# A feed-forward stage whose resident matmul operands lie at four offsets within 256 bytes

## The chip, the cores and the metric

The kernel runs on one core of one Trainium2 chip. The metric is the device time of one execution in microseconds; the median of several executions counts. Everything is float32 in the interface; the large matmuls run on operands that are split into a rounded high part and a remainder.

## The reference, cut to what matters

One encoder layer of width 1024 over 2048 positions. A mixer (convolution, gated recurrence and chunked attention side by side) comes first, then a gated feed-forward part of inner width 2816. The change lies in the feed-forward part alone:

```
mod = (c_act @ w_ada[l] + b_ada[l])[:, None, :]
sh1, sc1, g1, sh2, sc2, g2 = jnp.split(mod, 6, axis=-1)
...
x = layer_norm(ALPHA * x + (1.0 + g1) * y, ln1_g[l], ln1_b[l])
h = x * (1.0 + sc2) + sh2
gt, up = jnp.split(h @ w_ffn_in[l], 2, axis=-1)
y = (jax.nn.silu(gt) * up) @ w_ffn_out[l]
x = layer_norm(ALPHA * x + (1.0 + g2) * y, ln2_g[l], ln2_b[l])
```

## The kernel before

The program is traced as one long list of instructions with priorities, and a scheduler orders it on each engine; semaphores and places in memory are given by the same layer. The mixer takes the 2048 positions in four stretches of 512. Its projections are in `proj_f` (line 270: weights `whl` stationary, the input `hh`/`hl` moving, 512 columns) and `proj_t` (line 321: `hh`/`hl` or the mixer's output `yh`/`yl` stationary, weights `whl` moving, 256 columns).

Every float32 product is made of three matmuls, in the order of `PASSES`: high by high, high by low, low by high. A matmul names two operands in the core's memory: the stationary one (128 columns, loaded by its own weight load while the matmul before it streams) and the moving one (512 columns here, streamed through the array).

The feed-forward part has two stages.

- **First stage, `ffn_in` (line 953).** For each of two halves `g` of the positions and each of 22 blocks `f` of the inner width, seven products (a fast scheme for a 2 by 2 block product) are formed. Each product runs over four inner blocks `idx` and three passes, so a block has 7 x 4 x 3 = 84 matmuls and the stage 44 x 84 = 3696. The moving operands are `oph` and `opl`, the split activations; they stay resident for all 22 blocks of a half. The stationary operands are `fhi` and `flo`, the split weights, renewed for each block.
- **Second stage, `ffn_out` (line 1095).** For each of two halves `dh` of the output columns and each group `ts` of four (at the end two) blocks of positions, 22 inner blocks `f` are summed. The moving operands are the split output weights, which take the same tiles `oph`/`opl` through `load_op`, with `f % 4` as index; the stationary ones are `ahi`/`alo`, the split activations (for a few of the last group, `oph`/`opl` tiles as well).

`op_tiles` (line 853) asks for the resident tiles: one tag for each `idx` and part, with seven buffers of 2 KB per partition each, in the pool `p1`, which lies at the upper end of the memory and is filled from `idx` 0 upwards. The pools `st` (staging of the first stage) and `p2` (of the second) lie right below `p1`, `pw` (weights, `fhi`, `flo`, `fraw`, `fu`) lies at the lower end. All tiles here are a multiple of 512 bytes, so within one pool all start at the same offset modulo 256 bytes, as the built program gives them:

```
tiles                        offset modulo 256, before
oph, opl  (all 56 buffers)   224
fhi, flo, ahi, alo           160
st: opraw, h2, fraw0, xst    224
whl, hh, hl (mixer)          224
yh, yl (mixer)               192
```

The slices that a matmul reads within these tiles begin at multiples of 512 bytes, so these numbers hold for every matmul of lines 270, 321, 953 and 1095.

Of the kernel before, what the change touches and what calls it, by code (L numbers as in the profile page):

```python
# [7 lines left out]
F32 = mybir.dt.float32  # L8
# [7 lines left out]
P = 128  # L16
# [17 lines left out]
NK, NG = KT // 2, 2  # L34
# [74 lines left out]
def mixer_phase(tc, es, env):  # L109
# [681 lines left out]
    for q in range(NQ):  # L791
# [25 lines left out]
        if q + 1 == NQ:  # L817
            for _ in rest:
                pass
            as_.close()  # L820
            rs_.close()
            ffn_open(tc, env)
        else:
            nxt = fronts_a(q + 1)
# [7 lines left out]

def ffn_open(tc, env):
    pf = env["pf"] = ExitStack()
    env["p1"] = pf.enter_context(tc.tile_pool(name="p1", bufs=1, side="right", reuse_waits="tile"))
    st = env["st_es"] = ExitStack()
    env["st"] = st.enter_context(tc.tile_pool(name="st", bufs=1, side="right", reuse_waits="tile"))
    env["actd"] = [tc.dram_tile([P, NG * 2 * Q], F32, name=f"actd{f}") for f in range(NF)]
    env["ops"] = load_ops(tc, env, 0, range(2))
# [13 lines left out]
def op_tiles(env, idx):  # L853
    p1 = env["p1"]
    hi = p1.tile([P, Q], F32R, name="oph", tag=f"oph{idx}", bufs=7)
    lo = p1.tile([P, Q], F32R, name="opl", tag=f"opl{idx}", bufs=7)
    return hi, lo
# [10 lines left out]
def load_ops(tc, env, g, ns=range(7)):  # L868
    return {(n, idx): load_op(tc, env, env["srcd"][g][n * NK + idx], idx, env["st"], "h2", N_H2)
            for n in ns for idx in range(NK)}  # L870
# [344 lines left out]
```

## Time and profile before

| what | value |
|---|---|
| median of 3 runs | 2593.28 us (2588.7 to 2594.78) |
| the profiled execution | 2589.91 us |
| its span | 2588.2 us, granted clock 0.974 in the mean |
| PE busy | 2457.8 us, 95% of the span |
| DVE, ACT, POOL busy | 64%, 39%, 26% |
| the chain that ended last | PE 78%, of which line 953 31% and line 1095 17% |

Busy time of PE counts a matmul from its start to the end of its drain, and matmuls overlap. How fast they follow each other is read from the distance of their starts, in the timeline or from a count over a stretch without waits.

### The profile page before, as it was taken

How to read it: one execution, taken by the hardware profiler on the slowest of the kernel's cores; microseconds unless marked ns; L12 is line 12 of the kernel's file. 1: busy time of each engine (PE TensorE's matmuls, PEld its weight loads, DVE VectorE, ACT ScalarE, POOL GpSimd, SP SyncE). 2: the span in 40 equal slices, each digit the busy share in tenths (PEclk: the TensorE clock that was granted, in tenths of full speed). 3: DMA queues.
4: the chain of work that ended last, by engine and by line, in shares of the span. 5: the costliest groups of instructions: out<-in, count | busy, mean ns of one | idle time of the engine just before them, and what ended most of it. 6: DMA issues, size and time to landing. Idle time of an engine off the chain costs nothing.

```text
span 2588.2 us, 36360 instructions
## 1 busy us (share of the span) xinstructions
PE 2457.8 (95%) x13274; PEld 2078.5 (80%) x13274; DVE 1656.1 (64%) x2917; ACT 997.2 (39%) x1920; POOL 665.7 (26%) x571
## 2 busy tenths in 40 slices
PE   6888899999999999987999999999999999999998
PEld 5766799879977898876878788888888888888887
DVE  7987696669557785666655555765445474364666
ACT  2444444354244433544323333433333352242333
POOL 3433112200152112510333332332322211111121
PEclk8997999999999999988999999999999999999999
DMA  9676667663755645547333332442222274454544
GB/s 354 212 236 187 186 197 264 201 180 128 241 183 172 205 164 184 191 135 259 102 117 119 118 130 90 164 142 91 74 82 90 74 244 142 130 182 134 161 147 142
DMA packets 202691, 423.99 MB, mean 164 GB/s; under 512 B 20240, under 2 KB 69008, under 8 KB 202512
## 3 DMA queue, kind: packets, MB, share of 16 engines
q1 hardware_dynamic: 202352, 421.15, 49.8%
q8 instruction: 104, 1.70, 0.3%
q14 instruction: 75, 0.61, 0.1%
q0 software_dynamic: 160, 0.52, 0.1%
HBM read 317.78 MB, written 95.42 MB: 160 GB/s over the span
## 4 chain that ended last, share of the span: by engine, by line
PE 78%; DVE 10%; DMA 6%; issue 3%; ACT 2%; POOL 1%; SPq 0%; DVEq 0%; POOLq 0%; ACTq 0%
PE pi L953 31%; PE po L1095 17%; PE pjt L270 11%; PE pjt L321 9%; PE lp L513 2%; DVE cacc L377 2%; PE sc L625 1%; PE tp L661 1%; PE tp L648 1%; DMA whl<-wki 1%; DMA whl<-wko 1%; PE lp L533 1%; DMA xst<-zall 1%; DMA opraw<-srcd 1%; DMA xb<-in_x_dram 1%
## 5 line engine op out<-in xcount | busy, mean ns | idle before, releaser
L953 PE MATMUL pi<-oph,fhi 128*128 128x512 f32 x1232 | 484.1, 393 | 17.8 <-ACT fhi L829 11.9
L953 PE MATMUL pi<-opl,fhi 128*128 128x512 f32 x1232 | 483.7, 393 | 0.0
L953 PE MATMUL pi<-oph,flo 128*128 128x512 f32 x1232 | 478.9, 394 | 0.0
L270 PE MATMUL pjt<-hh,whl 128*128 128x512 f32 x1184 | 402.5, 411 | 16.2 <-DMA whl<-wki 6.4
L953 PEld LDWEIGHTS pi<-oph,fhi 128*128 128x128 f32 x1232 | 232.4, 189 | 70.2 <-ACT fhi L829 12.1
L829 ACT CAST fhi<-fraw 128x512 fp32r<-128x512 f32 x220 | 136.2, 621 | 392.3 <-PE pi L953 376.6
L270 PEld LDWEIGHTS pjt<-hh,whl 128*128 128x128 f32 x1184 | 227.4, 194 | 66.4 <-DMA whl<-wki 6.0
L958 DVE TENSOR_TENSOR fu<-fu,pi 128x512 f32<-128x512 f32 x176 | 120.8, 686 | 245.8 <-PE pi L953 245.1
L953 PEld LDWEIGHTS pi<-opl,fhi 128*128 128x128 f32 x1232 | 232.5, 189 | 52.3
L1095 PE MATMUL po<-oph,alo 128*128 128x512 f32 (+1 forms) x702 | 273.9, 390 | 0.0
L1095 PE MATMUL po<-oph,ahi 128*128 128x512 f32 (+1 forms) x702 | 270.1, 385 | 3.1 <-DVE res L1116 3.1
L1095 PE MATMUL po<-opl,ahi 128*128 128x512 f32 (+1 forms) x702 | 272.6, 388 | 0.0
L953 PEld LDWEIGHTS pi<-oph,flo 128*128 128x128 f32 x1232 | 232.3, 189 | 49.5 <-DVE flo L830 0.2
L830 DVE TENSOR_TENSOR alo<-araw,ahi 128x512 fp32r<-128x512 f32 x172 | 148.5, 871 | 190.9 <-ACT ahi L829 174.3
L270 PE MATMUL pjt<-hl,whl 128*128 128x512 f32 x592 | 243.0, 411 | 0.0
L321 PE MATMUL pjt<-whl,yh 128*128 128x256 f32 x1024 | 196.7, 288 | 15.5 <-DMA whl<-wko 12.0
L830 DVE TENSOR_TENSOR flo<-fraw,fhi 128x512 fp32r<-128x512 f32 x220 | 159.5, 742 | 70.9 <-ACT fhi L829 70.8
L377 DVE SCALAR_TENSOR_TENSOR cacc<-u,cs,cacc 128x512 f32<-128x512 f32 x240 | 195.3, 843 | 0.2
L829 ACT CAST ahi<-araw 128x512 fp32r<-128x512 f32 x172 | 104.9, 618 | 222.3 <-PE po L1095 208.0
L321 PEld LDWEIGHTS pjt<-whl,yh 128*128 128x128 f32 x1024 | 164.1, 194 | 17.7 <-DVE yl L231 7.9
L930 POOL TENSOR_TENSOR ft<-fraw 128x512 f32<-128x512 f32 x43 | 59.9, 1392 | 450.6 <-DMA fraw<-in_w_fi_dram 433.5
L1095 PEld LDWEIGHTS po<-oph,ahi 128*128 128x128 f32 x702 | 132.4, 189 | 31.7 <-DVE res L1116 3.3
(257 smaller groups left out, 4539.1 us busy)
## 6 DMA issues: line engine op xcount, KB each, us to landing
whl<-wki SPq DMA_DIRECT2D x156, 512.0 KB, 3.8
fraw<-in_w_fi_dram SPq DMA_DIRECT2D x86, 512.0 KB, 3.7
araw<-actd SPq DMA_DIRECT2D x154, 256.0 KB, 3.4
wki<-whl SPq DMA_DIRECT2D x52, 512.0 KB, 4.3
whl<-wko SPq DMA_DIRECT2D x48, 512.0 KB, 3.5
actd<-fs SPq DMA_DIRECT2D x44, 512.0 KB, 3.3
xb<-in_w_ada_dram SPq DMA_DIRECT2D x64, 256.0 KB, 4.7
opraw<-srcd SPq DMA_DIRECT2D x56, 256.0 KB, 5.0
```

The source lines that it names most:

```text
L270: nc.tensor.matmul(out=ps[j], lhsT=w[kt // 2][a][:, kt % 2, j * P:(j + 1) * P], rhs=hts[kt][c], start=(kt == 0 and n == 0), stop=(kt == KT ...
L321: nc.tensor.matmul(out=ps[tt // 2][:, tt % 2, :], lhsT=lhs[2 * kp + k][c][:, tt * P:(tt + 1) * P], rhs=w[kp][a][:, k, :], start=(ko == 0 a ...
L377: nc.vector.scalar_tensor_tensor(out=ac, in0=us[j][:, t:t + Q], scalar=col(wc + t), in1=ac, op0=ALU.mult, op1=ALU.add)
L513: nc.tensor.matmul(out=lp[0:n, c, :], lhsT=ddf[:, c * P:c * P + n], rhs=d4[:, c, :, :], start=True, stop=True)
L533: nc.tensor.matmul(out=lp[:, c, :], lhsT=K[:, 2 * i + c, :], rhs=M[:, 2 * i + c, :], start=True, stop=True)
L625: nc.tensor.matmul(out=sc[:, 0:n + x], lhsT=qs[hd][ph][:, i * P:(i + 1) * P], rhs=kt_[:, o - x0:o - x0 + n + x], start=ph == 0, stop=ph == 1)
L829: nc.scalar.copy(out=hi, in_=src)
L830: nc.vector.tensor_tensor(out=lo, in0=src, in1=hi.bitcast(F32), op=ALU.subtract)
L930: e.tensor_tensor(out=t1, in0=w12, in1=w11, op=ALU.subtract)
L953: nc.tensor.matmul(out=out, lhsT=w[n][a][:, idx, :], rhs=ops[n, idx][c], start=first and idx == 0 and i == 0, stop=idx == NK - 1 and i == ...
L958: nc.vector.tensor_tensor(out=out, in0=a, in1=b, op=ALU.add)
L1095: nc.tensor.matmul(out=pts[j][:, c], lhsT=a[x][:, j * P:(j + 1) * P], rhs=wo[f][y][:, c], start=f == 0 and m == 0, stop=f == NF - 1 and m ...
```

## The change

In `ffn_open` the pool `p1` is filled in an order and with spacers written out by hand. For each `idx` its two tags are asked for once, before their first use; ahead of `idx` 1, 2 and 3 stands a tile of 32 bytes per partition, and after the last a tile of 128 bytes. Nothing reads or writes the spacers, nor the eight tiles asked for here.

```
 def ffn_open(tc, env):
     pf = env["pf"] = ExitStack()
-    env["p1"] = pf.enter_context(tc.tile_pool(name="p1", bufs=1, side="right", reuse_waits="tile"))
+    p1 = env["p1"] = pf.enter_context(tc.tile_pool(name="p1", bufs=1, side="right", reuse_waits="tile"))
+    for idx in range(NK):
+        if idx:
+            p1.tile([P, 8], F32, name=f"gap{idx}")
+        op_tiles(env, idx)
+    p1.tile([P, 32], F32, name="gap")
     st = env["st_es"] = ExitStack()
```

In the built program the pool grows by 3 x 32 + 128 = 224 bytes, downwards:

```
tiles                        before   after   (modulo 256)
oph, opl, idx 0              224      0
oph, opl, idx 1              224      32
oph, opl, idx 2              224      64
oph, opl, idx 3              224      96
fhi, flo, ahi, alo           160      160
st: opraw, h2, fraw0, xst    224      0
```

Each engine has the same instructions on the same operands in the same order as before. One wait is new: the third GpSimd operation of the first weight block (line 937 before, `fraw0` in `st`) also waits for the last attention matmul of the mixer (line 661), since the pool `st` now overlaps other old tiles.

## Rows read from the trace of the kernel before

**Rows 1.** The page: busy time of each engine, and shares of the last chain.
```profile
PE 2457.8 (95%) x13274; PEld 2078.5 (80%) x13274; DVE 1656.1 (64%) x2917; ACT 997.2 (39%) x1920; POOL 665.7 (26%) x571
PE pi L953 31%; PE po L1095 17%; PE pjt L270 11%; PE pjt L321 9%; PE lp L513 2%; DVE cacc L377 2%; PE sc L625 1%; PE tp L661 1%; PE tp L648 1%; DMA whl<-wki 1%; DMA whl<-wko 1%; PE lp L533 1%; DMA xst<-zall 1%; DMA opraw<-srcd 1%; DMA xb<-in_x_dram 1%
```
**Rows 2.** Windows: stretch, length, busy time (instructions) by engine, granted clock, DMA.
```profile
1500.00:2100.00 600.00, 600.00 (x2630) 492.04 (x2629) 327.94 (x454) 212.63 (x363) 178.66 (x125) 1.00 0.33 113
```
**Rows 3.** Chain of work that ended last: start us, us, what.
```profile
1536.83 549.61 PE pi L953 x2400
...
2095.13 427.81 PE po L1095 x1869
```
**Rows 4.** Waits from 1500 us to 2588 us: waiter, awaited, us, times, longest.
```profile
ACT fhi L829 <- PE pi L953: 344.9, 187, 2.1
...
DVE fu L958 <- PE pi L953: 180.7, 83, 4.0
```
**Rows 5.** The same stretch, waits of PE alone.
```profile
PE po L1095 <- DVE res L1116: 3.1, 1, 3.1
```
**Rows 6.** Counts: windows of line 953 and 1095; casts into oph; groups by shape.
```profile
1227.00:2095.00 868.00, 855.16 (x3696) 695.65 (x3696) 0.99 0.33 112
...
2086.20:2580.50 494.30, 485.95 (x2178) 401.09 (x2178) 1.00 0.51 159
...
L829 ACT CAST oph<-opraw x100: 602/620/627, 1189.4 to 2323.0; 128x512 fp32r<-128x512 f32 x100
...
L1095 PE MATMUL po<-oph,ahi 128*128 128x256 f32 x28 | 8.6, 306 | 3.1 <-DVE res L1116 3.1
...
L1095 PE MATMUL po<-opl,oph 128*128 128x256 f32 x16 | 4.5, 282 | 0.0
```
**Rows 7.** Timeline of PE in line 953: start us, us, engine, line, what.
```profile
1700.13 0.39 PE L953 MATMUL pi<-oph,flo 128*128 128x512 f32 x1
...
1700.82 0.39 PE L953 MATMUL pi<-oph,flo 128*128 128x512 f32 x1
```
**Rows 8.** Timeline of PE in line 270, from the end of a wait.
```profile
851.94 0.50 PE L270 MATMUL pjt<-hh,whl 128*128 128x512 f32 x1 [0.47 <-DMA whl<-wki]
852.28 0.40 PE L270 MATMUL pjt<-hl,whl 128*128 128x512 f32 x1
...
854.61 0.62 PE L270 MATMUL pjt<-hh,whl 128*128 128x512 f32 x2
...
858.68 0.39 PE L270 MATMUL pjt<-hh,whl 128*128 128x512 f32 x1
```
**Rows 9.** Line 270 in a stretch of matmuls without a wait.
```profile
809.12 0.39 PE L270 MATMUL pjt<-hl,whl 128*128 128x512 f32 x1
...
817.28 0.39 PE L270 MATMUL pjt<-hl,whl 128*128 128x512 f32 x1
```
**Rows 10.** Timeline of PE in line 321, stationary yh and yl.
```profile
384.07 0.40 PE L321 MATMUL pjt<-whl,yh 128*128 128x256 f32 x2
...
384.77 0.40 PE L321 MATMUL pjt<-whl,yh 128*128 128x256 f32 x2
```
**Rows 11.** Timeline of PE in line 321, stationary hh and hl.
```profile
890.98 0.40 PE L321 MATMUL pjt<-whl,hh 128*128 128x256 f32 x2
...
891.70 0.40 PE L321 MATMUL pjt<-whl,hh 128*128 128x256 f32 x2
```
**Rows 12.** GpSimd at the first weight block: timeline, and its sequencer's wait.
```profile
1230.45 2.20 POOL L937 TENSOR_TENSOR fraw<-fraw,ft 128x512 f32<-128x512 f32 x1 [7.01 <-issue]
...
L937 POOLq EVENT_SEMAPHORE  x1: 7612/7612/7612, 1222.7 to 1222.7; - x1
```
**Rows 13.** The last attention matmuls (chain), and transposes of the first stage (line 889).
```profile
1179.73 1.29 PE tp L661 x20
...
L889 PE MATMUL tp<-ident,xst x64: 270/272/273, 1285.4 to 1536.6; 128*128 128x128 f32 x64
```

## The prediction

> **What bounds the kernel now.** I read the page first: PE is busy 95% of the span, and lines 953 and 1095, the two stages whose moving operands are moved in memory, hold 31% and 17% of the last chain [rows 1]. Is PE there the bound, or does it only happen to be late? From 1500 to 2100 us it is busy 600.00 of 600.00 us at a granted clock of 1.00, the 2.4 GHz level, while DVE, ACT and GpSimd are busy 328, 213 and 179 us [rows 2]. The waits of that stretch to the end run the other way: ACT and DVE wait for PE's matmuls (344.9 and 180.7 us in the first stage alone) [rows 4], PE itself for one result of DVE, 3.1 us [rows 5]. So what a matmul costs there goes to the end one for one, and a faster or slower matmul finds nothing that hides it: the other engines have slack on the fast side, and on the slow side they wait longer.
>
> How long is a matmul? Not its 388 to 394 ns in the groups, which include the drain, but the distance of starts. The chain gives it: 2400 matmuls of line 953 in 549.61 us, 229.0 ns each, and 1869 of line 1095 in 427.81 us, 228.9 ns [rows 3]. The timeline shows the same close up: three matmuls, one of each pass, in 0.69 us [rows 7]. At the full clock 512 columns need 512 / 2.4 = 213.3 ns. **So 15.6 ns of each matmul, 6.8%, are spent on something else than columns, though nothing is waited for.** That is the only thing that this change can touch.
>
> **Is it a matter of addresses?** The trace of before has two comparisons. First, line 321, where only the stationary operand differs: with `yh`/`yl` (offset 192) six matmuls of 256 columns take 0.70 us, 116.7 ns each [rows 10]; with `hh`/`hl` (offset 224, like the moving `whl`) they take 0.72 us, 120.0 ns [rows 11]. The code, shapes and clock are the same, the offset modulo 256 isn't. Second, line 270, where both operands lie at 224: 36 matmuls of 512 columns in 8.16 us, 226.7 ns [rows 9], against 228.9 in line 953 with 224 moving and 160 stationary. So an effect of 2 to 3 ns per matmul comes with the pair of offsets, of the order of a matmul's overhead, not of its length. I take it that the two reads, the moving one and the next weight load, which overlap, disturb each other, and that it depends on where they begin; the trace shows the difference, not the cause.
>
> A third reading speaks of how it sets in. In line 270, just behind a DMA wait, the first ten matmuls from 852.28 to 854.61 us are 233 ns apart, and the eighteen from there to 858.68 us 226 ns [rows 8]. The pattern needs some ten matmuls to settle.
>
> The Trainium skill speaks against the change here: "SBUF — State Buffer", section "Who interferes with whom", gives TensorE two independent read ports, one for the moving operand and one for the weight load, and says that TensorE never waits on anyone. By that page offsets would do nothing; the 116.7 against 120.0 ns do not agree with it, at least not without another cause. Its result is a rival below.
>
> **The change, part by part.**
>
> *The moving operands of line 953.* 3696 matmuls [rows 6], from 224 to 0, 32, 64 and 96 by inner block; the stationary ones stay at 160, so the difference of the two (moving less stationary) goes from 64 to 96, 128, 160 and 192 modulo 256. No row has these pairs. The nearest rows are 226.7 ns (difference 0) and 228.9 ns (difference 64, now), at 512 columns; the present pair is the worse of the two that are known in a settled state. The bounds are 213.3 ns, columns alone, and the unsettled 233 ns. I take 226.7, the value that a settled pattern at another difference has here: 3696 x 2.2 = 8.1 us less.
>
> *The moving operands of line 1095.* 2178 matmuls [rows 6]. In the last group some are of 256 columns: 28 for each of three pairs of names with `ahi`/`alo`, 16 for each of three with `oph`/`opl` as stationary operand, 132 in all [rows 6], so 2046 are full. The output weights use the same tiles, with f modulo 4 as index, so they move as well. 2046 x 2.2 = 4.5 us less. The 132 half-width ones change by 3.3 ns at most by rows 10 and 11: 0.4 us either way, left out.
>
> *The pool below.* `st` and `p2` go from 224 to 0. They feed casts of ACT (100 at 620 ns in the whole stage [rows 6]) and DVE, which lie under PE, and 64 transposes of line 889 [rows 13]; even 3 ns on each of those would be 0.2 us. Nothing.
>
> *The eight extra tiles and four spacers.* No instruction belongs to them; the buffers' turn begins one further, and the resident operands' waits stay. Nothing.
>
> *The new wait.* GpSimd's third operation on the first weight block starts at 1230.45 us, after its sequencer had stood for 7.6 us from 1222.7 us; the matmul that it must now also wait for ended by 1181.0 us [rows 12, 13]. The wait is met 40 us before. Queued behind it on GpSimd are this operation and the next of the block, and ACT's cast for PE's third product waits on them; an extra sequencer instruction there costs a fraction of a microsecond, below the rounding of the sum. If this cover were gone, the whole front of line 953 would stand.
>
> The sum is 8.1 + 4.5 = 12.6 us. From the profiled execution, 2589.91 us, that gives 2577.3 us. The median shown lies 3.4 us higher; against it the time is 2580.7 us, and that is what I give.
>
> **The rivals.**
>
> *Unsettled (slower).* In line 953 the offset now changes after every three matmuls, in line 1095 after every twelve or six. If a change of offset starts the pattern afresh as a wait does in rows 8, it never settles in 953 and hardly in 1095. Between the 231 ns that a half-settled pattern would have and the 233 of the first ten lies +2.1 to +4.1 ns on 5742 matmuls: 12 to 24 us slower, 2605 to 2617 us. It decides from the point where the mean passes 229 ns. For it: the change of offset every 0.7 us, and three of the four new differences are unlike any that has a row. Against it: in rows 8 a gap in the stream went ahead, and here there is none. The same time would come from differences that settle badly.
>
> *Nothing (same).* The offsets don't matter in this pairing, because the cost is per matmul, or because four differences average out to what one costs today. Then 2593 us, within 5 us. This is also what the Trainium skill's two independent ports say, on the page named above. For it: 228.9 and 226.7 lie only 1% apart, so averaging could well end between them. Against: the 3.3 ns between rows 10 and 11.
>
> *Much better (faster).* The present 15.6 ns are for the most part a clash of the two reads, and the new differences keep them apart, so that a matmul comes near its columns: 224 to 216 ns, 5 to 13 ns on 5742, 29 to 75 us less, 2518 to 2564 us. For it: all moving operands of 512 columns in this trace begin at 224, so none that begins at 0 or 64 was ever seen, and the overhead is large. Against it: no row at all below 226.
>
> [...]
>
> **How the numbers follow.** The forecast, 226.7 ns with about 1.2 ns to each side (6 to 19 us faster, 2574 to 2587 us): 0.38. Much better: 0.15. Nothing: 0.20. Unsettled: 0.27. Faster by over 0.2% (5 us, about what a measurement of this kernel can tell from no change) is the first two, 0.53; within it 0.20; slower 0.27. The range goes to half of the strong gain (41 us, 221.7 ns: 2552 us) and to 19 us on the slow side (232.2 ns: 2612 us), which leaves out some 0.08 on either end. The likeliest case's own range is 2574 to 2587 us.
>
> **What would show it.** In the profile after, line 953's chain row: 2400 matmuls in 544 us mean that the forecast's size is right, 549 us that nothing happened, 556 us or more that the pattern stays unsettled, 530 us that the reads really were in each other's way. Lines 270 and 321 must not change at all, since their operands don't move: if they do, it is not the offsets. In the timeline of line 953 the distances should repeat every twelve matmuls, as the offset goes round. The front at 1230 us should stand where it does. I am wrong in the mechanism if 953 and 1095 move in opposite directions by much, and in the sign if the four offsets cost more in passing from one to the next than each saves.

## Result: slower by 0.7%, and the profile after

| | before | changed |
|---|---|---|
| median of 3 runs | 2593.28 us | 2607.78 us (2604.8 to 2611.15) |
| ratio | 1 | 1.0067, 95% interval 1.0048 to 1.0086 |
| span of the profiled execution | 2588.2 us | 2609.4 us |

The forecast was 2580.7 us, faster; the kernel is 14.5 us slower by the medians. The range of 2552 to 2612 us holds the time, the sign is the other one. The spans differ by more than the medians, 21.2 us: the profiled execution of the changed kernel is the slowest of its three, and single executions of one kernel scatter. Of the kernel before, 24 executions beside the first experiments lie between 2580.73 and 2599.31 us, with a median of 2589.84 us, 17.9 us below the changed kernel. How fast the matmuls follow each other is therefore read from the traces, where it repeats far more closely: 549.61 and 549.35 us for 2400 matmuls in before and in e4 below, which have the same offsets there.

PE is still what everything waits for. The stretch from 1500 to 2100 us of the changed kernel answers to [rows 2]: stretch, length, busy time of PE, weight load, DVE, ACT and GpSimd, granted clock, DMA share, GB/s.

```profile
1500.00:2100.00 600.00, 600.00 (x2593) 485.37 (x2592) 319.24 (x440) 203.14 (x346) 171.30 (x121) 1.00 0.31 106
```

The clock is the same full 2.4 GHz level and PE is busy throughout, but 2593 matmuls stand where 2630 stood. To the end of the program PE waits once, as in [rows 5]:

```profile
PE po L1100 <- DVE res L1121: 1.5, 1, 1.5
```

The chain of the changed kernel (start us, us, what; lines 958 and 1100 are 953 and 1095 of before) answers to [rows 3]:

```profile
1544.03 557.38 PE pi L958 x2400
...
2110.24 447.31 PE po L1100 x1917
```

557.38 / 2400 = 232.2 ns and 447.31 / 1917 = 233.3 ns between starts, where before had 229.0 and 228.9. The sum by the prediction's own counts is 3696 x 3.2 + 2046 x 4.4 = 11.8 + 9.0 = 20.8 us, against 21.2 us between the two spans. So nearly the whole loss between the two spans stands in the two stages, in matmuls that wait for nothing.

The front is where it was. The chain and the sequencer's rows of GpSimd in the changed kernel answer to [rows 12, 13]:

```profile
1180.67 1.29 PE tp L661 x20
...
1230.91 2.12 POOL fraw L942
```
```profile
L942 POOLq EVENT_SEMAPHORE  x2: 17/30/43, 1230.7 to 1230.8; - x2
```

The last attention matmuls end at 1182.0 us, and the operation that now also waits for them starts at 1230.91, against 1230.45 us before: the new wait costs nothing.

### The profile page after: what moved, and what is told of

The parts are those of the page before. It is cut to its first block, busy times and chain, and to the rows that moved or that the text cites. A ratio compares the mean times of both kernels' runs of the same rounds, so it can differ in the third digit from the quotient of the medians.

```text
span 2609.4 us, 36361 instructions
## 1 busy us (share of the span) xinstructions
PE 2476.6 (95%) x13274; PEld 2075.0 (80%) x13274; DVE 1656.4 (63%) x2917; ACT 997.5 (38%) x1920; POOL 666.0 (26%) x571
## 4 chain that ended last, share of the span: by engine, by line
PE 75%; DVE 13%; DMA 7%; issue 2%; ACT 2%; POOL 1%; SPq 1%; DVEq 0%; ACTq 0%; POOLq 0%
PE pi L958 31%; PE po L1100 18%; PE pjt L270 10%; PE pjt L321 7%; DVE cacc L377 3%; PE lp L513 2%; PE sc L625 1%; DMA xb<-in_w_ada_dram 1%; PE tp L661 1%; PE tp L648 1%; DMA whl<-wki 1%; DMA xst<-zall 1%; DVE tmp L496 1%; DVE tmp L297 1%; PE lp L533 1%
## 5 line engine op out<-in xcount | busy, mean ns | idle before, releaser
L958 PE MATMUL pi<-oph,fhi 128*128 128x512 f32 x1232 | 488.8, 397 | 19.6 <-ACT fhi L829 13.1
L958 PE MATMUL pi<-opl,fhi 128*128 128x512 f32 x1232 | 490.3, 398 | 0.0
L958 PEld LDWEIGHTS pi<-opl,fhi 128*128 128x128 f32 x1232 | 233.1, 189 | 54.4
```

The lines of the kernel that those rows point to most:

```text
L958: nc.tensor.matmul(out=out, lhsT=w[n][a][:, idx, :], rhs=ops[n, idx][c], start=first and idx == 0 and i == 0, stop=idx == NK - 1 and i == ...
```

## Experiments: which pair of offsets, and what a passing costs

Two explanations were open: the passing from one offset to the next (the prediction's slower rival), or each new pair of offsets by itself. All twelve kernels have the instructions of before in the same order on each engine; only places in memory differ (and the new wait, where the pools `st` and `p2` move). A difference below is the moving operand's offset less the stationary one's, modulo 256 bytes.

### One offset instead of four

Experiment e1 keeps the changed kernel's pool and its size, without the spacers between the inner blocks, so that all lie at 0.

```
-    env["p1"] = pf.enter_context(tc.tile_pool(name="p1", bufs=1, side="right", reuse_waits="tile"))
+    p1 = env["p1"] = pf.enter_context(tc.tile_pool(name="p1", bufs=1, side="right", reuse_waits="tile"))
+    for idx in range(NK):
+        op_tiles(env, idx)
+    p1.tile([P, 56], F32, name="gap")
```

> The four inner blocks lie at one offset, 0 modulo 256, for moving operands; the stationary ones stay at 160; staging is at 0 as in the changed kernel. Theory 'pair' (the time of a matmul is set by the offsets of its two operands, and settles at once): both stages at 233 ns between starts, as line 1095 of the changed kernel has within its runs of twelve at offset 0, so 15 to 25 us slower than before. Theory 'unsettled' (the passing from one offset to the next costs): 227 to 229 ns, within 12 us below or level with before.

Measured: 2610.29 us, ratio 1.0077 (1.0052 to 1.0102). Its chain:

```profile
1540.79 560.00 PE pi L956 x2400
...
2109.66 447.54 PE po L1098 x1918
```

233.3 ns in both stages, with nothing to pass between. So a passing is not needed for the loss: the pair of offsets alone brings it.

### The stationary operands moved to the moving ones

Experiment e2 leaves the resident operands at 224 and puts 64 bytes ahead of the split weights (the other tiles of `pw` behind them move along).

```
     pw.tile([P, 2, NK, P], F32, name="fraw", tag="fraw", bufs=N_RAW)
+    pw.tile([P, 16], F32, name="wgap")
```

> The kernel before with a spacer of 64 bytes ahead of the split weights: moving operands at 224, stationary at 224 instead of 160. Theory 'difference' (what counts is the difference of the two offsets, as line 270 with 224 and 224 shows): 226.7 ns in both stages, 12 to 13 us faster than before. Theory 'start of the moving operand' (only that offset counts): 228.9 ns, no change.

Measured: 2576.78 us against 2589.84 us of before beside it, ratio 0.9951 (0.9935 to 0.9967).

```profile
1530.55 544.04 PE pi L953 x2400
...
2083.21 423.65 PE po L1096 x1869
```

544.04 / 2400 = 226.7 and 423.65 / 1869 = 226.7 ns, as line 270 in [rows 9]. The gain is 3696 x 2.3 + 2046 x 2.2 = 13.0 us by the chain and 13.1 us by the medians. This is the size of gain that was forecast for the change (12.6 us), from an edit that makes the two offsets equal.

Experiment e3 puts both at 0: e1 with a `wgap` of 24 floats as in e2.

> Moving operands of all four inner blocks at 0 and the stationary ones at 0 as well. Theory 'difference': the difference is 0 as in line 270, so 226.7 ns and 12 to 13 us faster than before. Theory 'start of the moving operand': 0 is the bad place, so 233 ns and 15 to 25 us slower, as with all at 0 and the stationary ones at 160.

Measured: 2576.72 us, ratio 0.9948 (0.9929 to 0.9967).

```profile
1528.58 544.05 PE pi L956 x2400
...
2081.24 423.65 PE po L1099 x1869
```

Again 226.7 ns, at a place where e1 had 233.3 with the same moving operands. So the start of the moving operand doesn't decide, its distance from the stationary one does. Against e2 the moving operands lie 256 bytes further back from the stationary ones; this is the one place where it is tested that only the difference modulo 256 bytes counts. In e2 and e3 the other tiles of `pw` move too, and no run moves those alone; but in e1, and in e10 to e12 below, `pw` stays where it was and the time changes all the same. e2 and e3 beat both kernels.

### The staging alone

Experiment e4 moves only what lies below the resident tiles, with a spacer of 224 bytes in a pool of its own between `p1` and `st`.

```
     env["p1"] = pf.enter_context(tc.tile_pool(name="p1", bufs=1, side="right", reuse_waits="tile"))
+    sp = pf.enter_context(tc.tile_pool(name="sp", bufs=1, side="right"))
+    sp.tile([P, 56], F32, name="gap")
     st = env["st_es"] = ExitStack()
```

> Only the staging pools below the resident tiles move by 224 bytes, to offset 0, and the one new wait comes with them; both matmul operands stay where they were before. Both theories: no change, 228.9 ns in both stages and a time within 5 us of before. If it is 10 us or more slower, the cost lies in the staging or the new wait and not in the matmuls' operands.

Measured: 2586.54 us, ratio 0.9992 (0.9972 to 1.0012), 549.35 us for 2400 matmuls in the first stage and 439.02 us for 1918 in the second, 228.9 ns in both.

```profile
1533.96 549.35 PE pi L955 x2400
...
2092.01 439.02 PE po L1097 x1918
```

The staging and the new wait have no part in it.

### The other differences

Experiment e5 is e2 with 8 floats (stationary at 192, difference 32), e6 with 24 (stationary at 0, difference 224).

> The kernel before with a spacer of 32 bytes ahead of the split weights: stationary operands at 192, moving at 224, so their difference (moving less stationary) is 32, which no run of 512 columns had so far. Theory 'difference grows with distance': between the 226.7 ns at 0 and the 228.9 ns at 64, 5 to 13 us faster than before. Theory 'line 321' (there a difference of 32 took 116.7 ns where 0 took 120.0 at 256 columns, so 32 is the best place): below 226.7 ns, 13 to 30 us faster than before.

> The kernel before with a spacer of 96 bytes ahead of the split weights: stationary operands at 0, moving at 224, so the difference is 224, that is 32 the other way round. Theory 'the sign doesn't count, only the distance': as with the stationary ones at 192. Theory 'everything from 96 to 224 is bad, since the moving read, which is the faster, then starts behind the weight load's and runs into it': about 233 ns, 15 to 25 us slower than before.

Measured: e5 2614.72 us, ratio 1.0099 (1.0084 to 1.0114); e6 2609.6 us, ratio 1.008 (1.0061 to 1.0099). The chain of e5:

```profile
1542.53 560.00 PE pi L953 x2400
...
2111.39 447.55 PE po L1096 x1918
```

And of e6:

```profile
1695.76 408.37 PE pi L953 x1749
...
2112.99 446.93 PE po L1096 x1916
```

Both lie at 233.3 to 233.5 ns (in e6 PE waited once, 0.93 us, just ahead of the first row). Neither "between" nor "best place" held for 32: a step of 32 bytes away from equal offsets, to either side, costs all of the 6.7 ns. That line 321 of the kernel before is the faster with a difference of 32 is true of 256 columns and false of 512.

The runs so far leave open three of the four pairs of the changed kernel. Experiments e10 to e12 are e1 with 48, 40 and 32 floats in the last spacer, so that all inner blocks lie at 32, 64 and 96: these three pairs, one at a time, each in a single execution.

> All inner blocks at 32, the stationary operands at 160, difference 128: the second of the four pairs of the changed kernel by itself. Theory 'the pair sets it': 233 ns in both stages, as within the runs of twelve at this offset in line 1095 of the changed kernel. Theory 'passing': 227 to 229 ns once nothing passes from one offset to another.

> All inner blocks at 64, the stationary operands at 160, difference 160: the third pair of the changed kernel by itself. Theory 'the pair sets it': 233 to 234 ns in both stages. Theory 'passing': 227 to 229 ns.

> All inner blocks at 96, the stationary operands at 160, difference 192, that is 64 the other way round from before: the fourth pair of the changed kernel by itself. Theory 'the pair sets it': 233 ns in both stages. Theory 'only the distance counts, not the sign': 228.9 ns as before, and then the changed kernel's time would need another cause for this quarter.

Measured: 2605.63, 2613.15 and 2609.49 us, against one execution of before beside them with 2586.43 us. With the scatter given above, the rows of the chain say more than these times. The chains, e10 first:

```profile
1537.74 557.72 PE pi L956 x2400
```

e11:

```profile
1538.97 562.28 PE pi L956 x2400
```

e12:

```profile
1539.77 560.00 PE pi L956 x2400
```

That completes the circle in steps of 32 bytes, all at 512 columns and the full clock, from the chain's first-stage rows (the second stage agrees within 0.3 ns):

| difference, bytes | offsets (moving, stationary) | ns between starts | from |
|---|---|---|---|
| 0 | 224, 224 and 0, 0 | 226.7 | e2, e3 |
| 32 | 224, 192 | 233.3 | e5 |
| 64 | 224, 160 | 229.0 | before, [rows 3] |
| 96 | 0, 160 | 233.3 | e1 |
| 128 | 32, 160 | 232.4 | e10 |
| 160 | 64, 160 | 234.3 | e11 |
| 192 | 96, 160 | 233.3 | e12 |
| 224 | 224, 0 | 233.5 | e6 |

The changed kernel uses 96, 128, 160 and 192, four of the six bad ones; their mean is 233.3 ns, and it has 233.3 in the second stage and 232.2 in the first. The sign of the difference counts as well: 64 is good, and 192, which is 64 the other way round, is bad. The reason that was offered with e6, that all from 96 to 224 is bad, does not cover 32, which is just as bad.

### What a passing costs

In experiment e7 inner blocks 0 and 1 lie at 160 (difference 0) and 2 and 3 at 224 (difference 64), the two good places.

```
-    env["p1"] = pf.enter_context(tc.tile_pool(name="p1", bufs=1, side="right", reuse_waits="tile"))
+    p1 = env["p1"] = pf.enter_context(tc.tile_pool(name="p1", bufs=1, side="right", reuse_waits="tile"))
+    for idx in range(NK):
+        if idx == 2:
+            p1.tile([P, 16], F32, name="gap")
+        op_tiles(env, idx)
```

> Inner blocks 0 and 1 lie at 160, like the stationary operands (difference 0), blocks 2 and 3 at 224 (difference 64): two places, each known by itself (226.7 and 228.9 ns), with a passing between them after every six matmuls in line 953. If the passing costs nothing: 227.8 ns, 6 us faster than before. If each passing costs a settling as behind a wait: 230 ns or more in line 953, 4 us slower or worse, and less in line 1095, where it comes after 24 matmuls.

Measured: 2593.78 us, ratio 1.0020 (1.0004 to 1.0035).

```profile
1532.94 554.48 PE pi L957 x2400
...
2096.19 438.98 PE po L1099 x1917
```

231.0 ns in the first stage, where the mean of the two pairs is 227.8: 3.2 ns on each of the six matmuls between passings, some 19 ns for a passing. In the second stage, with 24 matmuls between most passings, 229.0 ns; there the timeline shows each passing by itself:

```profile
2202.78 0.40 PE L1099 MATMUL po<-oph,ahi 128*128 128x512 f32 x1
...
2203.72 0.39 PE L1099 MATMUL po<-opl,ahi 128*128 128x512 f32 x1
...
2208.29 0.40 PE L1099 MATMUL po<-oph,ahi 128*128 128x512 f32 x1
...
2210.61 0.39 PE L1099 MATMUL po<-opl,ahi 128*128 128x512 f32 x1
...
2213.78 0.39 PE L1099 MATMUL po<-oph,ahi 128*128 128x512 f32 x1
```

At 2202.78 us the moving operands pass from 160 to 224: four matmuls take 0.94 us, 235 ns each, and the next twenty 4.57 us, 228.5 ns each, near the settled 229.0 of that pair. At 2208.29 us they pass back: ten matmuls take 2.32 us, 232 ns each, and the last fourteen 3.17 us, 226.4 ns each. Right behind the passing that is 4 x 6 = 24 ns more than settled one way and 10 x 5.3 = 53 ns the other. Over the whole round of 48 matmuls the two passings cost some 0.06 us, 11.00 us where the two settled pairs make 10.94. The settling that rows 8 show behind a wait is real for a change of offset too, here between two good pairs.

Experiment e8 is the change without its last spacer, so that the four offsets are 128 to 224 and the differences 224, 0, 32 and 64.

> The change without its last spacer: four offsets 128, 160, 192 and 224 with the stationary operands at 160, so differences of 224, 0, 32 and 64. Theory 'difference': the mean of the four, with two known (226.7 at 0, 228.9 at 64) and two from the runs beside this one (stationary at 192 and at 0), so 228 ns if both of these are near 228 and 229 if one is 233: within 6 us of before. Theory 'four offsets cost by themselves': 232 ns or more in line 953, 11 us or more slower than before.

Measured: 2599.23 us, ratio 1.0035 (1.0019 to 1.0051).

```profile
1539.98 555.29 PE pi L957 x2400
...
2104.13 432.66 PE po L1099 x1869
```

231.4 and 231.5 ns. The mean of its four pairs in the table is (233.5 + 226.7 + 233.3 + 229.0) / 4 = 230.6; 0.8 to 0.9 ns are left for the passing. That is 2 to 3 ns for each in the first stage, which passes every three matmuls, and some 11 in the second, which passes every twelve, so a passing has no fixed price. Neither expectation was right: two of its pairs are bad, and four offsets add little to that.

### The load beside, or the operands of the matmul itself

In experiment e9 the high parts of the weights lie at 224 and the low parts at 0, so that only the low parts are at a bad difference.

```
-    for k in ("fhi", "flo"):
+    for k, n in (("fhi", 16), ("flo", 8)):
+        pw.tile([P, n], F32, name=f"gap{k}")
         pw.tile([P, Q], F32R, name=k, tag=k, bufs=N_WOP)
```

> The high parts of the weights lie at 224 like the moving operands (difference 0), the low parts alone at 0 (difference 224, 233 ns in the run with all at 0). Of a figure of three passes only the third has a low part as its own stationary operand, and that one is loaded while the second streams. Theory 'own operands': high by high and high by low stay at 226.7 ns, only low by high grows. Theory 'clash with the load beside it': the second pass, high by low, during which the low part is loaded, grows, and the third stays near 226.7 ns. In either case the mean of line 953 lies between 226.7 and 233.3 ns, above 229 if each passing also costs a settling.

Measured: 2617.42 us in one execution, beside 2586.43 us of before; 559.42 us for 2400 matmuls, 233.1 ns. The groups by shape of e9 in the second stage (line, engine, operation, names, shapes, count, busy us, mean ns of one, idle us):

```profile
L1096 PE MATMUL po<-opl,ahi 128*128 128x512 f32 x674 | 269.6, 400 | 0.0
L1096 PE MATMUL po<-oph,ahi 128*128 128x512 f32 x674 | 266.2, 395 | 0.0
L1096 PE MATMUL po<-oph,alo 128*128 128x512 f32 x674 | 262.2, 389 | 0.0
```

And of e2, where all operands are at 224:

```profile
L1096 PE MATMUL po<-oph,ahi 128*128 128x512 f32 x674 | 262.2, 389 | 0.0
L1096 PE MATMUL po<-opl,ahi 128*128 128x512 f32 x674 | 262.2, 389 | 0.0
L1096 PE MATMUL po<-oph,alo 128*128 128x512 f32 x674 | 262.2, 389 | 0.0
```

The order of passes is `oph` with `ahi`, `opl` with `ahi`, `oph` with `alo`. The third, which has the low part as its own stationary operand, is as long as in e2, 389 ns. The second, beside which the low part is loaded, grows by 11 ns, and the first by 6, though the operands of both lie at 224. So a matmul can grow whose own two operands lie well, and the theory of the own operands fails.

That it is the load beside it which makes the second grow is not shown by this, however near it lies. In e1, where all operands of the three passes stand at one and the same difference, the three are uneven in the same way:

```profile
L1098 PE MATMUL po<-opl,ahi 128*128 128x512 f32 x674 | 268.9, 399 | 0.0
L1098 PE MATMUL po<-oph,ahi 128*128 128x512 f32 x674 | 265.6, 394 | 0.0
L1098 PE MATMUL po<-oph,alo 128*128 128x512 f32 x674 | 264.2, 392 | 0.0
```

There too the second pass is the longest, and no load lies apart. So which of the three grows does not tell which read disturbed it. What e9 shows is that the pairs don't add up one by one: one stationary operand of three at a bad difference costs as much (233.1 ns) as all three (233.3 to 233.5 ns in e6).

## Why the prediction was wrong

**What bounds the kernel: right.** Every nanosecond on a matmul of the two stages went to the end: 20.8 us from the counts, 21.2 us in the span.

**That offsets matter, and by their pair: right**, and now shown by e1 against e3: the same moving operands, 233.3 or 226.7 ns. That the two reads disturb each other, which the prediction took for the cause, is still not shown. The Trainium skill's "SBUF — State Buffer", section "Who interferes with whom", says that TensorE's two read ports are independent and that it never waits on anyone; the runs do not agree, with 6.7 ns between the best and a bad pair. By that page e1 and e3 would have taken the same time, and they differ by 34 us. The rival "nothing", 2593 us, fell: the changed kernel's rows stand 3.2 and 4.4 ns above those of before.

**The step that failed** is the term for line 953: "I take 226.7, the value that a settled pattern at another difference has here", taken over into line 1095. It let the one equal pair that the trace held stand for four differences that no row showed. Measured: 233.3, 232.4, 234.3 and 233.3 ns for these four. The bound on that side, 233 ns, was there and nearly right, but it came from an unsettled stretch and was read as a passing state; in these pairs it is the lasting one. The term came out as 232.2 - 229.0 = +3.2 ns instead of -2.2, the one of line 1095 as +4.4.

The prediction gives one ground for the term: the present pair was the worse of the two that were known in a settled state. That was true, and said nothing of the six others: it is the second best of eight. Nor could rows 10 and 11, where a difference of 32 beats a difference of 0, have led further. At 512 columns it is the reverse, 233.3 against 226.7 (e5, e2): a row of another shape gave the existence of the effect, and not its direction.

**The rival "unsettled"** named 2605 to 2617 us, and the median is 2607.78. Its mechanism is not the reason: without any passing the time is the same (e1). But its last sentence, "The same time would come from differences that settle badly", names what the runs then showed. It was given no chance and no sign of its own. A passing does cost some 20 to 50 ns between two good pairs (e7); in the changed kernel nothing of it is seen, and the first stage, which passes every three matmuls, is even 1.1 ns below the mean of its pairs. By the sign that the prediction set for it, 556 us or more in the chain's row, the 557.38 us would have been read as "unsettled"; e1, with 560.00 us and no passing, shows that the sign could not tell the two apart.

**"Much better"** fell: no run of 512 columns went below 226.7 ns, so of the 15.6 ns over the columns at least 13.4 remain at every difference tried. What they are was not found.

**The sign condition of the last part**, "wrong in the sign if the four offsets cost more in passing from one to the next than each saves", missed the real one, that each might cost by itself.

**The smaller terms** held: staging and wait nothing (e4), the front where it stood, and lines 270 and 321 all but unmoved (their largest groups have means of 411 and 411, 288 and 286 ns). In the changed kernel's first stage the distances of starts do repeat every twelve matmuls, in one settled stretch 233, 230, 237, 232, 234, 237, 230, 229, 236, 235, 235 and 232 ns, 2.80 us in sum: the offset going round is seen. In other stretches another sequence of twelve recurs, with a sum of 2.78 us, and the mixture of both gives the 232.2 ns.

## What to carry to other kernels

Where PE streams without a wait and the distance of starts is still above the columns' time, look at where the two operands begin: equal offsets modulo 256 bytes were the best of eight settings for 512 columns of four bytes, and a spacer of 64 bytes bought 0.5%. An effect of placement that a trace shows for one pair and one shape says that there is an effect, not which way the next pair goes; all the steps of the circle have to be tried, one uniform setting at a time, before settings are mixed. Spreading operands over several offsets is then no hedge, since most of them may be bad and a passing between good ones costs a settling (e7). And a rival that would give the same time by another cause needs a sign of its own, set beforehand, or the time will be taken as proof of the wrong one.

## What the runs showed of the hardware

A matmul of 512 columns, at the full granted clock and with nothing to wait for, settles at a mean of 226.7, 229.0 or 232.4 to 234.3 ns, and the difference of its moving operand's start to that of the stationary operands chooses among them: 0, 64, and all else in steps of 32 bytes. Only for a difference of 0 was this tried at two places (e2, e3). With 256 columns the order of 0 and 32 is reversed (120.0 and 116.7 ns, [rows 10, 11]). A change of difference between the two good settings costs some 20 ns one way and some 50 the other (e7). The pairs don't add up one by one: one stationary operand in three at a bad difference costs as much as all (e9). Smaller steps than 32 bytes were not tried; which read disturbs which, and how, stays open.
